# Layer 1's up products of the feed-forward: both parts of the state as one moving operand of 512 columns

## The chip, the cores and the metric

The kernel runs on one core of a Trainium2 chip. The metric is the device time of one execution in microseconds (us): the median of several runs. Three runs of the kernel before gave 1219.34, 1221.35 and 1221.39 us, median 1221.35.

## What is computed

Two layers of a block over 256 latent tokens (and, in layer 0 alone, 256 context tokens) of width 1024. Each layer mixes tokens in four branches and then applies a gated feed-forward, which is the part that the change touches:

```
def swiglu(h, w_up, w_down):
    a, u = jnp.split(h @ w_up, 2, axis=-1)
    return (jax.nn.silu(a) * u) @ w_down
```

with `w_up` of 1024 x 5632 and `w_down` of 2816 x 1024. Layer 1 is the last one: it has the 256 latent tokens only.

## The kernel before, in words

**Split numbers.** Products are taken in a reduced float format (fp32r), and accuracy is kept by splitting each operand x into a high part hi = x rounded to that format and a low part lo = x - hi. A product of w and h is then three products on TensorE into one PSUM bank: hi(w) hi(h), hi(w) lo(h), lo(w) hi(h) (`mm3`, lines 220 to 224). For a weight block the split is done on the chip: `_split` (line 97) issues a ScalarE copy for hi (line 102) and, through `flush` (line 108), a VectorE subtraction for lo (line 112).

**The up stage of layer 1** (`ffn`, line 1206, with T = 256 columns and NS = 1). The 5632 output channels are 44 blocks of 128: 22 gate blocks f (the half called a above) and 22 value blocks NF + f (the half called u). They are worked in pairs: gate block f, then value block NF + f. A block is 8 chunks k of 128 channels of the state; each chunk is one `mm3` with moving operands of 256 columns (`up_mm`, line 1222), so 24 products and 24 weight loads per block. The result lies in one of three PSUM banks that rotate (tag "b"). After a gate block `up_a` (line 1237) takes the sigmoid on ScalarE (line 1239) and multiplies on VectorE (line 1240); after a value block `up_u` (line 1243) multiplies on VectorE (sf, line 1246) and splits sf into shi on ScalarE (line 211) and slo on VectorE (line 212). The state of this stage is hm1: `new_h` (line 492) makes 8 tiles for its high parts and 8 for its low parts, 256 columns each, which `modulate` (line 472) fills. The first pair of blocks is worked chunk by chunk as the state comes (lines 1295 to 1302).

**The down stage** takes 22 blocks of 12 products of 512 columns each, on other PSUM banks, and reads shi and slo.

**Order.** Each engine works its instructions in the order in which the program issues them. The program is a list of steps; before each one the planner (`Weights.pump`, line 114) issues what is due of loads and splits, and then the step's own function runs:

```
            more = self.split_to(self.nth + ahead) or more
        assert all(b.raw is not None and (b.hi is not None or not b.split) for b in blocks)
```

```
    for n, st in enumerate(steps):
        weights.pump(n, st.blocks, st.ahead, st.lag)
        st.fn()
```

With `ahead` = 2, which all the steps of whole blocks have, the split of block n+2 (hi on ScalarE, lo on VectorE) is issued ahead of the products of block n and of what follows them. The split parts live in four ring buffers, the raw weights in four others, which SP's queue fills (line 94).

Of the kernel before, what the change touches and what calls it, by code (L numbers as in the profile page):

```python
# [8 lines left out]
F32 = mybir.dt.float32  # L9
F32R = mybir.dt.float32r  # L10
BF16 = mybir.dt.bfloat16
AF = mybir.ActivationFunctionType
ALU = mybir.AluOpType
# [4 lines left out]
P = 128  # L18
D = 1024
KC = D // P  # L20
# [6 lines left out]
NF = DFF // P  # L27
# [138 lines left out]
def kernel(ctx: ExitStack, tc: tile.TileContext, a: dict, out: bass.AP):  # L166
    ctx.enter_context(tc.manual_schedule())
    nc = tc.nc

    def pool(name, bufs=1, stack=ctx, **kw):  # L170
        return stack.enter_context(tc.tile_pool(name=name, bufs=bufs, reuse_waits="tile", **kw))
# [5 lines left out]
    hp = pool("hp")  # L177
# [5 lines left out]
    def bank(tag, name, shape=None, keep=False):  # L183

        i = banks[tag].pop(0)
        if not keep:
            banks[tag].append(i)
        t = psum.tile([P, 512], F32, tag=f"bank{i}", name=name)
        return t if shape is None else cut(t, shape)
# [4 lines left out]
    def cut(t, shape):  # L194
        n = 1
        for x in shape:
            n *= x
        t = t[:, :n]
        if len(shape) == 2:
            t = t.rearrange("p (a b) -> p a b", b=shape[1])  # L200
        if len(shape) == 3:
            t = t.rearrange("p (a b c) -> p a b c", b=shape[1], c=shape[2])
        return t
# [6 lines left out]
    def split(hi, lo, src):  # L210
        nc.scalar.activation(hi, src, AF.Copy)
        nc.vector.tensor_tensor(lo, src, hi.bitcast(F32), op=ALU.subtract)
# [7 lines left out]
    def mm3(ps, st, mv, first, last):  # L220

        nc.tensor.matmul(ps, lhsT=st[0], rhs=mv[0], start=first, stop=False)  # L222
        nc.tensor.matmul(ps, lhsT=st[0], rhs=mv[1], start=False, stop=False)  # L223
        nc.tensor.matmul(ps, lhsT=st[1], rhs=mv[0], start=False, stop=last)  # L224
# [265 lines left out]
            cut_lows()  # L490

    def new_h(T, name):
        return [
            [hp.tile([P, T], F32R, tag=f"h{x}{k}", name=f"{name}{x}{k}") for k in range(KC)]
            for x in ("hi", "lo")
        ]
# [709 lines left out]
    def ffn(l, h, hnext, before, chains):  # L1206
        T = 512 if l == 0 else 256
        NS = T // SEQ
        outer, early, late = ExitStack(), ExitStack(), ExitStack()
        P_ = {}  # L1210
# [9 lines left out]
        pps = {}  # L1220

        def up_mm(blk, b, cols, tag, ks=range(KC)):
            if b not in pps:
                pps[b] = bank(tag, f"up{l}{b}")[:, :T]
            for k in ks:
                sl = slice(k * P, (k + 1) * P)
                mm3(
                    pps[b][:, cols],
                    (blk.hi[:, sl], blk.lo[:, sl]),
                    (h[0][k][:, cols], h[1][k][:, cols]),  # L1230
                    k == 0,
                    k == KC - 1,
                )

        sgs = {}

        def up_a(f):
            sg = P_["t"].tile([P, T], F32, tag="sg", name="fsg")
            nc.scalar.activation(sg, pps[f], AF.Sigmoid)
            nc.vector.tensor_tensor(sg, sg, pps[f], op=ALU.mult)  # L1240
            sgs[f] = sg

        def up_u(f):
            sg, u = sgs.pop(f), pps[NF + f]
            sf = P_["t"].tile([P, SEQ], F32, tag="sf", name="sf")
            nc.vector.tensor_tensor(sf, sg[:, :SEQ], u[:, :SEQ], op=ALU.mult)
            if NS == 2:
                sc = P_["s"].tile([P, SEQ], F32, name=f"sc{f}")
                nc.vector.tensor_tensor(sc, sg[:, SEQ:], u[:, SEQ:], op=ALU.mult)
                sc_.append(sc)  # L1250
            hi = P_["s"].tile([P, SEQ], F32R, name=f"shi{f}")
            lo = P_["s"].tile([P, SEQ], F32R, name=f"slo{f}")
            split(hi, lo, sf)
            sh_.append(hi)
            sl_.append(lo)

        def up_block(b):
            return Block(a["w_up"][l, b], f"up{l}{b}")

        fs = list(range(NF))  # L1260
        if NS == 2:
# [3 lines left out]
            for n, (f, b, blk) in enumerate(first):  # L1265
                ks = range(KC) if n < 3 else range(KC // 2)
                steps.append(Step([blk], lambda blk=blk, b=b, ks=ks: up_mm(blk, b, lat, "a", ks), free=[]))
            _, b3, blk3 = first[3]
            do(at(turn, 0), lambda: up_mm(blk3, b3, lat, "a", range(KC // 2, KC)), before, begin)

            def up_end(f, b):
                (up_a if b == f else up_u)(f)

            def up_ctx(k0):
                for _, b, blk in first[:2]:
                    up_mm(blk, b, ctx_, None, (k0, k0 + 1))
# [13 lines left out]
        else:  # L1290
# [9 lines left out]
            steps[-1].ahead = 0  # L1300
            do(before, begin)
            steps.append(Step([], lambda: (up_a(0), up_u(0)), free=[blk for _, blk in first]))
            fs = fs[1:]
        for f in fs:
            for b in (f, NF + f):
                blk = up_block(b)

                def fn(f=f, b=b, blk=blk):
                    up_mm(blk, b, slice(0, T), "b")
                    (up_a if b == f else up_u)(f)  # L1310

                steps.append(Step([blk], fn))
# [58 lines left out]
    h = {}  # L1371

    def get_h(key, T):
        def fn():
            if key not in h:
                h[key] = new_h(T, f"h{key}")
            return h[key]

        return fn
# [190 lines left out]
    start = next(i for i, st in enumerate(mix0) if st.tick)  # L1570
    steps = mix0[:start] + weave(mix0[start:], cond_rows() + gate_steps_of(0, 0, 2) + mod_steps(0, 1, 2), 21, 46)

    class Later:
# [5 lines left out]
        def __getitem__(self, i):  # L1579
            return h[self.key][i]  # L1580

    ff0, end1 = ffn(0, Later("m0"), get_h("f0", 512), end0, ch0)
    both = gate_steps_of(0, 1, 2) + mod_steps(1, 0, 2)
    lat_only = mod_steps(1, 1, 1) + gate_steps_of(1, 0, 1) + gate_steps_of(1, 1, 1)
    steps += weave(ff0, cond_rows() + mixed(both, lat_only), 5, 60)
    mix1, end2, ch1 = mixer(1, Later("f0"), get_h("m1", 256))
    mix1.insert(0, Step([], end1, tick=False))
    steps += mix1
    ff1, end3 = ffn(1, Later("m1"), None, end2, ch1)
    steps += ff1  # L1590

# [104 lines left out]
```

## Time and profile before

| what | value |
|---|---|
| median of 3 runs | 1221.35 us |
| the profiled execution's own time | 1220.89 us |
| its span, first to last instruction | 1219.1 us |
| granted clock of TensorE, mean | 0.995 |
| TensorE busy | 98% of the span |
| VectorE busy | 783.1 us, 64% |
| ScalarE busy | 453.2 us, 37% |
| layer 1's up stage | about 1025 to 1152 us of the span |
| layer 1's down stage | about 1152 to 1212 us |

Times in rows are microseconds from the span's start. PE is TensorE (its products), PEld its weight loads, DVE VectorE, ACT ScalarE, SP the engine that issues transfers. "L112" is line 112 of the kernel; tiles go by the program's names, so `lo_up` is the low part of an up block and `fsg` the gate's result. Busy times of products overlap, because a product's row lasts from its first read to its modelled end: how fast TensorE goes is read from the steps between starts.

### The profile page before, as it was taken

The page shows a single profiled execution, that of the slowest core. Times are in us where ns is not written, and L with a number is a line of the kernel's source. Part 1 is how long each engine was busy: PE and PEld are TensorE (multiplying, and loading weights), DVE is VectorE, ACT ScalarE, POOL GpSimd, SP SyncE. Part 2 cuts the span into 40 slices and gives each one's busy share as a digit, 9 for nine tenths or more (in the row PEclk, how much of TensorE's full clock was granted, in tenths as well). Part 3 has the DMA queues.
Part 4 walks back from the last instruction along what each step waited for, and adds up shares of the span by engine and source line. Part 5 has one row for each costly group of instructions (what it writes and reads, how often), then busy time and mean ns, then how long its engine had stood idle before and what let it go on. Part 6 is the DMA issues. An engine that isn't in the chain of part 4 may idle for free.

```text
span 1219.1 us, 17611 instructions
## 1 busy us (share of the span) xinstructions
PE 1189.1 (98%) x6960; PEld 1028.8 (84%) x6960; DVE 783.1 (64%) x1275; ACT 453.2 (37%) x715; POOL 41.7 (3%) x39
## 2 busy tenths in 40 slices
PE   7999999999999989999999999989989999999997
PEld 5987778888888878888888888889879998999986
DVE  5464745586875656775777673576666666666644
ACT  4332323323222643222322222564334445444442
POOL 1500000000000100000000000000000000000000
PEclk9999999999999999999999999999999999999999
DMA  8642325457565225666666773334455663665662
GB/s 290 233 131 70 112 87 190 150 180 172 183 194 161 67 104 170 210 204 169 233 204 215 245 234 97 130 111 160 125 155 163 199 233 112 191 183 181 201 214 86
DMA packets 66435, 205.67 MB, mean 169 GB/s; under 512 B 14640, under 2 KB 18480, under 8 KB 66352
## 3 DMA queue, kind: packets, MB, share of 16 engines
q1 hardware_dynamic: 65776, 204.39, 53.6%
q8 instruction: 55, 0.90, 0.3%
q14 instruction: 28, 0.23, 0.1%
q10 hardware_dynamic: 576, 0.16, 0.1%
HBM read 203.41 MB, written 1.11 MB: 168 GB/s over the span
## 4 chain that ended last, share of the span: by engine, by line
PE 87%; DVE 5%; ACT 4%; DMA 2%; issue 2%; POOL 1%; SPq 0%; DVEq 0%; POOLq 0%; ACTq 0%
PE up L223 10%; PE up L224 10%; PE up L222 10%; PE gate L222 7%; PE gate L224 7%; PE gate L223 7%; PE dn L224 4%; PE dn L223 4%; PE dn L222 4%; PE pb L224 2%; PE pb L223 2%; PE pb L222 2%; PE wo L224 1%; ACT junk L443 1%; PE wo L223 1%
## 5 line engine op out<-in xcount | busy, mean ns | idle before, releaser
L338 DVE SCALAR_TENSOR_TENSOR mjunk<-raw_mod,crow 128x1024 bf16<-128x1024 f32 x128 | 156.4, 1222 | 8.8 <-DMA raw_mod<-in_w_modt 6.8
L223 PE MATMUL up<-hm0lo,hi_up 128*128 128x512 f32 (+1 forms) x384 | 143.5, 374 | 2.8 <-DVE hm0lo L470 2.8
L224 PE MATMUL up<-hm0hi,lo_up 128*128 128x512 f32 (+1 forms) x384 | 143.2, 373 | 2.5 <-DVE lo_up L112 2.5
L222 PE MATMUL up<-hm0hi,hi_up 128*128 128x512 f32 (+1 forms) x384 | 143.5, 374 | 0.0
L112 DVE TENSOR_TENSOR lo_up<-raw_up,hi_up 128x1024 fp32r<-128x1024 f32 x88 | 107.6, 1223 | 36.6 <-ACT hi_up L102 36.5
L112 DVE TENSOR_TENSOR lo_gt<-raw_gt,hi_gt 128x1280 fp32r<-128x1280 f32 x64 | 95.3, 1489 | 31.4 <-ACT hi_gt L102 31.4
L222 PE MATMUL gate<-h0hi,hi_gt 128*128 128x512 f32 x256 | 100.6, 393 | 0.0
L222 PE MATMUL up<-hm1hi,hi_up 128*128 128x256 f32 x352 | 99.8, 284 | 0.0
L223 PE MATMUL up<-hm1lo,hi_up 128*128 128x256 f32 x352 | 99.7, 283 | 0.1
L223 PE MATMUL gate<-h0lo,hi_gt 128*128 128x512 f32 x256 | 99.6, 389 | 0.0
L224 PE MATMUL gate<-h0hi,lo_gt 128*128 128x512 f32 x256 | 99.6, 389 | 0.0
L224 PE MATMUL up<-hm1hi,lo_up 128*128 128x256 f32 x352 | 99.6, 283 | 0.0
L102 ACT ACTIVATE hi_up<-raw_up 128x1024 fp32r<-128x1024 f32 x88 | 92.2, 1049 | 9.5 <-DMA raw_up<-in_w_up 8.9
L102 ACT ACTIVATE hi_gt<-raw_gt 128x1280 fp32r<-128x1280 f32 x64 | 81.0, 1265 | 21.1 <-DMA raw_gt<-in_w_gate 21.0
L112 DVE TENSOR_TENSOR lo_dn<-raw_dn,hi_dn 128x1024 fp32r<-128x1024 f32 x44 | 53.6, 1224 | 54.1 <-ACT hi_dn L102 54.1
L223 PEld LDWEIGHTS up<-hm0lo,hi_up 128*128 128x128 f32 x384 | 72.8, 190 | 16.0 <-DVE hm0lo L470 3.7
L224 PEld LDWEIGHTS up<-hm0hi,lo_up 128*128 128x128 f32 x384 | 72.9, 190 | 15.3 <-DVE lo_up L112 2.7
L1065 ACT ACTIVATE sg<-gate 128x512 f32<-128x512 f32 (+1 forms) x64 | 31.3, 488 | 143.6 <-PE gate L224 143.5
L222 PEld LDWEIGHTS up<-hm0hi,hi_up 128*128 128x128 f32 x384 | 72.9, 190 | 12.5
L102 ACT ACTIVATE hi_dn<-raw_dn 128x1024 fp32r<-128x1024 f32 x44 | 46.4, 1058 | 91.8 <-PE dn L224 68.3
L222 PE MATMUL gate<-hf0hi,hi_gt 128*128 128x256 f32 x256 | 73.5, 287 | 0.0
L223 PE MATMUL gate<-hf0lo,hi_gt 128*128 128x256 f32 x256 | 72.4, 283 | 0.0
(342 smaller groups left out, 2718.3 us busy)
## 6 DMA issues: line engine op xcount, KB each, us to landing
raw_up<-in_w_up SPq DMA_DIRECT2D x88, 512.0 KB, 3.9
raw_gt<-in_w_gate SPq DMA_DIRECT2D x64, 640.0 KB, 3.9
raw_mod<-in_w_modt SPq DMA_DIRECT2D x80, 512.0 KB, 4.1
raw_dn<-in_w_down SPq DMA_DIRECT2D x44, 512.0 KB, 4.3
raw_in<-in_w_in SPq DMA_DIRECT2D x28, 512.0 KB, 3.7
raw_wo<-in_w_o SPq DMA_DIRECT2D x16, 512.0 KB, 4.1
raw_mod<-in_w_mod SPq DMA_DIRECT2D x12, 512.0 KB, 5.2
grow<-gscr SPq DMA_DIRECT2D x6, 512.0 KB, 7.2
```

What stands on the lines that cost most here:

```text
L102: self.nc.scalar.activation(b.hi, b.raw, AF.Copy)
L112: self.nc.vector.tensor_tensor(b.lo, b.raw, b.hi.bitcast(F32), op=ALU.subtract)
L222: nc.tensor.matmul(ps, lhsT=st[0], rhs=mv[0], start=first, stop=False)
L223: nc.tensor.matmul(ps, lhsT=st[0], rhs=mv[1], start=False, stop=False)
L224: nc.tensor.matmul(ps, lhsT=st[1], rhs=mv[0], start=False, stop=last)
L338: nc.vector.scalar_tensor_tensor(junk, b.raw, 1.0, crow[s], op0=ALU.mult, op1=ALU.mult, accum_out=out()[:, s, i : i + 1])
L443: nc.scalar.activation(junk, src, AF.Square, scale=1.0 / 32.0, accum_out=acc)
L1065: nc.scalar.activation(sg, ps, AF.Sigmoid)
```

## The change

In layer 1 alone, the high and the low part of each state chunk become the two halves of one tile of 512 columns (`new_h`). A chunk is then two products: hi(w) with all 512 columns into a whole PSUM bank, and lo(w) with the 256 columns of the high part into the bank's first half; in the last chunk in the other order. The bank's second half thus holds hi(w) lo(h) by itself, and `up_sum` adds the halves: a ScalarE copy of the second half into SBUF and a VectorE addition of the first. The sigmoid and both multiplications then read the sum in SBUF instead of PSUM. Layer 0 keeps its products.

```diff
     def new_h(T, name):
+        if name == "hm1":
+
+            hl = [hp.tile([P, 2 * T], F32R, tag=f"hhi{k}", name=f"{name}{k}") for k in range(KC)]
+            return [[x[:, :T] for x in hl], [x[:, T:] for x in hl], hl]
         return [
...
         def up_mm(blk, b, cols, tag, ks=range(KC)):
             if b not in pps:
-                pps[b] = bank(tag, f"up{l}{b}")[:, :T]
+                pps[b] = bank(tag, f"up{l}{b}")
             for k in ks:
                 sl = slice(k * P, (k + 1) * P)
+                if NS == 1:
+                    run = [(pps[b], blk.hi, h[2][k]), (pps[b][:, :T], blk.lo, h[0][k])]
+                    for n, (ps, w, x) in enumerate(run[::-1] if k == KC - 1 else run):
+                        nc.tensor.matmul(ps, lhsT=w[:, sl], rhs=x, start=k == 0 and n == 0, stop=k == KC - 1 and n == 1)
+                    continue
                 mm3(
...
+        def up_sum(b):
+
+            if NS == 2:
+                return pps[b]
+            x = P_["t"].tile([P, T], F32, tag="us", name="fus")
+            nc.scalar.activation(x, pps[b][:, T:], AF.Copy)
+            nc.vector.tensor_tensor(x, x, pps[b][:, :T], op=ALU.add)
+            return x
+
         def up_a(f):
+            x = up_sum(f)
             sg = P_["t"].tile([P, T], F32, tag="sg", name="fsg")
-            nc.scalar.activation(sg, pps[f], AF.Sigmoid)
-            nc.vector.tensor_tensor(sg, sg, pps[f], op=ALU.mult)
+            nc.scalar.activation(sg, x, AF.Sigmoid)
+            nc.vector.tensor_tensor(sg, sg, x, op=ALU.mult)
             sgs[f] = sg
 
         def up_u(f):
-            sg, u = sgs.pop(f), pps[NF + f]
+            sg, u = sgs.pop(f), up_sum(NF + f)
```

## Rows read from the trace of the kernel before

**Rows 1.** The page: span, and each engine's busy us (share) and instructions.

```profile
span 1219.1 us, 17611 instructions
...
PE 1189.1 (98%) x6960; PEld 1028.8 (84%) x6960; DVE 783.1 (64%) x1275; ACT 453.2 (37%) x715; POOL 41.7 (3%) x39
```

**Rows 2.** Windows, up stage: us, busy PE, PEld, DVE, ACT, POOL, clock, DMA share, GB/s.

```profile
1031.10:1152.40 121.30, 121.30 (x1013) 121.30 (x1012) 79.14 (x107) 56.92 (x85) 0.00 (x0) 1.00 0.62 186
```

**Rows 3.** Timeline of PE in layer 0's up stage: start, duration, line, operation.

```profile
559.76 0.39 PE L222 MATMUL up<-hm0hi,hi_up 128*128 128x512 f32 x1
...
569.96 0.39 PE L222 MATMUL up<-hm0hi,hi_up 128*128 128x512 f32 x1
```

**Rows 4.** Timeline of PE where 512 columns are followed by 256.

```profile
416.35 0.39 PE L224 MATMUL wo<-hi_wo,ml 128*128 128x512 f32 x1
416.58 0.28 PE L222 MATMUL up<-hm0hi,hi_up 128*128 128x256 f32 x1
416.70 0.28 PE L223 MATMUL up<-hm0lo,hi_up 128*128 128x256 f32 x1
```

**Rows 5.** Groups by line, 880 us to the end: count, busy us, mean ns, idle before.

```profile
L223 PEld LDWEIGHTS up<-hm1lo,hi_up 128*128 128x128 f32 x352 | 67.6, 192 | 0.3 <-DVE hm1lo L470 0.3
```

**Rows 6.** Timeline of DVE, one pair of blocks; brackets hold idle time and its releaser.

```profile
1034.17 1.23 DVE L112 TENSOR_TENSOR lo_up<-raw_up,hi_up 128x1024 fp32r<-128x1024 f32 x1 [0.53 <-ACT hi_up L102]
1035.31 0.42 DVE L1240 TENSOR_TENSOR fsg<-fsg,up 128x256 f32<-128x256 f32 x1
1035.91 1.23 DVE L112 TENSOR_TENSOR lo_up<-raw_up,hi_up 128x1024 fp32r<-128x1024 f32 x1 [0.19 <-ACT hi_up L102]
1037.43 0.42 DVE L1246 TENSOR_TENSOR sf<-fsg,up 128x256 f32<-128x256 f32 x1 [0.29 <-PE up L224]
1038.34 0.43 DVE L212 TENSOR_TENSOR slo<-sf,shi 128x256 fp32r<-128x256 f32 x1 [0.48 <-ACT shi L211]
1039.29 1.23 DVE L112 TENSOR_TENSOR lo_up<-raw_up,hi_up 128x1024 fp32r<-128x1024 f32 x1 [0.52 <-ACT hi_up L102]
```

**Rows 7.** Timeline of ACT over the same pair.

```profile
1034.55 0.38 ACT L1239 ACTIVATE fsg<-up 128x256 f32<-128x256 f32 x1 [0.41 <-PE up L224]
1034.83 1.05 ACT L102 ACTIVATE hi_up<-raw_up 128x1024 fp32r<-128x1024 f32 x1
1037.89 0.42 ACT L211 ACTIVATE shi<-sf 128x256 fp32r<-128x256 f32 x1 [2.00 <-DVE sf L1246]
1038.21 1.04 ACT L102 ACTIVATE hi_up<-raw_up 128x1024 fp32r<-128x1024 f32 x1
```

**Rows 8.** Timeline of DVE in layer 1's mixer, an operation that reads the last one's result.

```profile
945.55 0.41 DVE L1074 TENSOR_TENSOR sg<-sg,pb 128x256 f32<-128x256 f32 x1
946.00 0.43 DVE L1075 TENSOR_TENSOR mg<-mg,sg 128x256 f32<-128x256 f32 x1
```

**Rows 9.** Timelines of PE and DVE at the start of layer 1's up stage.

```profile
1025.31 0.38 PE L223 MATMUL up<-hm1lo,hi_up 128*128 128x256 f32 x1
...
1031.80 0.41 DVE L1240 TENSOR_TENSOR fsg<-fsg,up 128x256 f32<-128x256 f32 x1
1032.32 0.42 DVE L1246 TENSOR_TENSOR sf<-fsg,up 128x256 f32<-128x256 f32 x1
```

**Rows 10.** Timelines at the start of the down stage: DVE's lo, PE in block three.

```profile
1154.49 3.50 DVE L112 TENSOR_TENSOR lo_dn<-raw_dn,hi_dn 128x1024 fp32r<-128x1024 f32 x3 [0.53 <-ACT hi_dn L102]
...
1158.12 0.39 PE L223 MATMUL dn<-lo_dn,shi 128*128 128x512 f32 x1
```

**Rows 11.** DMA issues, 1030 to 1150 us: count, KB each, median us to landing.

```profile
raw_up<-in_w_up SPq DMA_DIRECT2D x38, 512.0 KB, 3.7
```

**Rows 12.** Windows as in rows 2, and PE's timeline in a stretch at half clock.

```profile
816.34 0.41 PE L223 MATMUL bg<-hf0lo,hi_in 128*128 128x256 f32 x1
...
818.47 0.41 PE L224 MATMUL bg<-hf0hi,lo_in 128*128 128x256 f32 x1
...
890.00:900.00 10.00, 8.66 (x70) 7.64 (x70) 6.40 (x13) 6.72 (x13) 0.00 (x0) 1.00 0.50 115
```

## The prediction

> **What bounds the kernel now.** I read the page first, then the stretch of layer 1's feed-forward cut out by time, then the timelines of the three engines that work in it. The page says that TensorE is busy for 98% of the span [rows 1]. In the stretch from 1031.1 to 1152.4 us, where 42 of the 44 up blocks of layer 1 are multiplied, it is busy all the time at the full granted clock (1.00, so 2.4 GHz), while VectorE has 79.1 us of work and ScalarE 56.9 us [rows 2]. So this stage is bound by TensorE today, and one is tempted to ask only what the change does to TensorE. The busy shares hide what matters here: VectorE and ScalarE work in the order of the program and hand work to each other, so that their chain can be much longer than either one's busy time.
>
> **TensorE's part of the change.** Today a chunk k of a block takes three products of 256 columns; after it, one of 512 and one of 256. The number of columns is the same (768). 1013 products of 256 columns fill 121.3 us [rows 2], 0.120 us each; 256 columns at 2.4 GHz are 0.1067 us, so 0.013 us of each is a fixed part. Products of 512 columns follow each other at (569.96 - 559.76)/45 = 0.2267 us (46 records, the two shown are the first and the last) [rows 3], which is 0.2133 + 0.013: the fixed part is per product, not per column. Where 512 columns are followed by 256 the steps are 0.23 and 0.12 us [rows 4], so mixing costs nothing that the row shows. A chunk goes from 3 x 0.120 = 0.360 to 0.2267 + 0.120 = 0.347 us, a block of eight from 2.88 to 2.77 us, and the 352 chunks [rows 5] save 352 x 0.0133 = **4.7 us of TensorE**. The bounds: nothing (a 512-column product at twice 0.120), and 352 x 0.120 = 42 us if a product's whole step went away, which the 0.2267 us of rows 3 exclude.
>
> 352 weight loads go too. Each row of one lasts 192 ns [rows 5], but it lies beside a product: with steps of 0.120 us there is no room for it outside. So I price a removed load at nothing beyond the 0.013 us above. The Trainium skill ("TensorE: Matmul & The Clock Gate", part 3, on what overlaps) says that a weight load overlaps products in flight only where it goes to another row group, which these full-size loads don't; with its price for a load, 128 columns at 1.2 GHz or 107 ns, TensorE would save 38 us by estimate. The steps of 0.120 us for products whose columns alone take 0.107 speak against it.
>
> **What is added on the other two engines.** Per block: a ScalarE copy of 128x256 from PSUM, and a VectorE addition of 128x256 with one operand in PSUM. The nearest rows are sf, a VectorE operation with the same kinds of operands (0.42 us) [rows 6], the sigmoid, which reads the same shape from PSUM (0.38), and the shi copy (0.42) [rows 7]. In busy time VectorE goes from 79.1/42 = 1.88 to 2.30 us a block, still under TensorE's 2.77. By busy time the addition would be hidden. It is not, because of where it stands in the queues.
>
> **The order in the queues.** At step n the planner first issues the split of block n+2 (hi on ScalarE, lo on VectorE, at once), then the products of block n, then what follows block n. The rows show it: lo, mult, lo, sf, slo, lo on VectorE [rows 6], and sigmoid, hi, shi, hi on ScalarE [rows 7]. Today the sigmoid waits for TensorE alone, so for a gate block ("a") the next hi doesn't depend on VectorE. For a value block ("u") it does: sf, shi, hi, lo. After the change it does **for every block**: the addition of block n stands on VectorE behind lo of block n+2; the sigmoid (a) or sf and shi (u) need its result; hi of block n+3 stands on ScalarE behind them; lo of n+3 needs that hi. The loop closes: lo(n+2), add(n), sigmoid or shi(n), hi(n+3), lo(n+3). The copy is outside of the loop, since ScalarE does it while lo runs.
>
> Its length, start to start:
> - lo to the next VectorE operation that waits for nothing: 1034.17 to 1035.31, 1.14 us [rows 6].
> - A VectorE result to a ScalarE start: sf 1037.43 to shi 1037.89, 0.46 us [rows 6, 7], taken for add to sigmoid too.
> - add to sf, both on VectorE, the second reading the first's result: 945.55 to 946.00, 0.45 us [rows 8]; the other end is 1031.80 to 1032.32, 0.52 us [rows 9].
> - sigmoid to hi 0.28 us, shi to hi 0.32 [rows 7]. The sigmoid will read SBUF as shi does, so 0.32 for both.
> - hi to lo: 1034.83 to 1035.91 and 1038.21 to 1039.29, 1.08 us [rows 6, 7].
>
> While the addition waits for lo, everything of its block stands behind it on VectorE, the next lo too, and TensorE waits for that one. A gate block: 1.14 + 0.46 + 0.32 + 1.08 = 3.00 us. A value block: 1.14 + 0.45 + 0.46 + 0.32 + 1.08 = 3.45 us. **A pair: 6.45 us**, against 5.54 us that TensorE needs for it after the change and 5.76 today. The same sum for today is 1.14 + 0.46 + 0.32 + 1.08 = 3.0 for the value block, and for the gate block 1.14 + 0.42, so 4.6 us a pair: hidden under 5.76. For the ends of the pair I take 6.30 (the sigmoid to hi at 0.28, and each hand-over a little shorter) and 6.65 (0.52 instead of 0.45, and as much more at two other hand-overs).
>
> **The sum.** The multiplication behind blocks 0 and 1 starts at 1031.80 [rows 9]; the first addition will start in its place (VectorE is busy with lo until then). Then sigmoid 1032.26, mult 1032.7, the second addition 1033.1, sf 1033.5, shi 1034.0, hi 1034.3, lo of block 4 at 1035.4, done at 1036.6. TensorE, done with blocks 0 and 1 at about 1031.1 (the start of the stretch [rows 2]), needs it two blocks later, at 1031.1 + 5.54 = 1036.6; from block 6 on it waits for the loop. Lo runs two blocks ahead, so the loop covers 21 pairs until lo of the third down block: 1035.4 + 21 x 6.45 = 1170.9, done 1.23 later, at 1172.1 us. Today the product that needs it (the second of that block) starts at 1158.12, long after its lo, which starts at 1154.49 [rows 10]. So the down products, and all behind them, start 14.0 us later. From there on VectorE has only one lo per 12 x 0.2267 = 2.72 us, and catches up. The profiled execution took 1220.9 us, 0.5 below the median of the three runs; 1220.9 + 14.0 = **1234.9, forecast 1235 us**. With 6.30 and 6.65 a pair the delay is 10.8 and 18.2 us: 1231.7 to 1239.1.
>
> The other edits. The state's parts in one tile: the very first product now waits for the low part, where only the second did, at 1025.31 [rows 9]; the wider product then ends where the second one does today, so nothing, and if that cover is gone at most that product's 0.38 us. A PSUM bank is free after the addition instead of after the product with it, and three banks rotate; TensorE waits for lo anyway, so nothing, and at most one VectorE operation, 0.42 us, per block once lo came early. Weight loads from memory land in 3.7 us for a block [rows 11] and there are four buffers for a block each 3.2 us: nothing, and SP's queue keeps its order.
>
> **The rivals.**
> 1. *The loop doesn't close, and TensorE stays the bound: faster.* It needs a pair under 5.54 us, that is additions that run ahead of lo on VectorE, or 0.9 us less in the hand-overs. For it: busy time alone (2.30 us a block) leaves room. Against it: the order in rows 6, where nothing overtakes a waiting lo. Time: 1220.9 - 4.7 = 1216 us. Chance 0.08. In 0.01 of these the loads removed are worth their whole row, 352 x 0.192 = 68 us [rows 5], which the steps of 0.120 speak against: 1153 us. The Trainium skill's rule above would put this case at 1183 us.
> 2. *The loop closes at TensorE's pace,* about 5.6 to 5.9 us a pair, because hand-overs are shorter or the fixed part of a product isn't saved: from -3 to +2 us, about 1221. Chance 0.04.
> 3. *TensorE's clock falls as well.* It will wait some 0.45 us in each 3.2. At 1.2 GHz a 256-column product takes (818.47 - 816.34)/10 = 0.213 us [rows 12], a block 8 x (0.427 + 0.213) = 5.1 us instead of 2.77, more than the loop. Were half of 40 blocks so, 20 x (5.1 - 3.2) = 38 us more: 1273 us; one block in eight, 10 us more, 1245. Against it: between 890 and 900 us TensorE was busy for 8.66 of 10 us, and the granted clock stayed at 1.00 [rows 12]. Chance 0.08, mostly at its lower end.
> 4. The forecast: 0.80.
>
> **Numbers.** 0.2% is 2.4 us, about what a measurement of this kernel can tell from no change. Faster 0.09 (rival 1 and a bit of 2), same 0.03 (the rest of 2), slower 0.88 (forecast and 3). The range takes the loop from just under 6.2 to 6.8 a pair, and leaves out rivals 1, 2 and the upper part of 3: 1228 to 1243 us.
>
> **What the next profile would show.** Right: TensorE's products of the up stage at steps of 0.227 and 0.12, but with a wait before nearly every block, put down to lo_up; VectorE idle before lo (for hi) and ScalarE idle before the sigmoid (for the addition); lo_up at alternating steps of 3.0 and 3.45 us; the stage some 14 us longer and the down stage as long as before. Wrong: no waits of TensorE for lo_up (rival 1), or a granted clock under 1 between 1040 and 1165 us (rival 3). A longer or shorter pair with the same waits would mean that a hand-over was mispriced.

## The result and the profile after

The changed kernel takes 1234.07 us, the median of four runs (1233.47 to 1234.67); the kernel before has a median of 1220.34 us over its four runs. The ratio is 1.0113, with a 95% interval of 1.01 to 1.0125: 13.7 us slower. The forecast was 1235.

The page of the changed kernel, its span and the busy line, as in [rows 1]:

```profile
span 1232.7 us, 16951 instructions
...
PE 1195.5 (97%) x6607; PEld 1007.4 (82%) x6608; DVE 797.8 (65%) x1319; ACT 465.4 (38%) x759; POOL 41.6 (3%) x39
```

The span has grown by 13.6 us, as the time has. VectorE and ScalarE have 14.7 and 12.2 us more of work spread over a stage of some 140 us, and neither is near full. The answer is not in this line. Who waited for whom between 1040 and 1165 us (total us, times, longest us):

```profile
...
ACT fsg L1258 <- DVE fus L1252: 25.8, 19, 1.4
PEld up L1234 <- DVE lo_up L112: 22.2, 38, 0.8
DVE lo_up L112 <- ACT hi_up L102: 20.0, 38, 0.5
DVE slo L212 <- ACT shi L211: 9.7, 20, 0.5
...
PE up L1234 <- DVE lo_up L112: 7.0, 18, 0.4
```

Two of these are new. The sigmoid (fsg) waits for VectorE's sum (fus), where it used to wait for TensorE. And TensorE waits for lo_up before 38 blocks, most plainly at its weight load. Now VectorE's timeline over one pair of blocks, to be laid beside [rows 6]:

```profile
1041.40 1.23 DVE L112 TENSOR_TENSOR lo_up<-raw_up,hi_up 128x1024 fp32r<-128x1024 f32 x1 [0.53 <-ACT hi_up L102]
1042.55 0.41 DVE L1252 TENSOR_TENSOR fus<-fus,up 128x256 f32<-128x256 f32 x1
1043.45 0.42 DVE L1259 TENSOR_TENSOR fsg<-fsg,fus 128x256 f32<-128x256 f32 x1 [0.48 <-ACT fsg L1258]
1044.40 1.23 DVE L112 TENSOR_TENSOR lo_up<-raw_up,hi_up 128x1024 fp32r<-128x1024 f32 x1 [0.53 <-ACT hi_up L102]
1045.54 0.41 DVE L1252 TENSOR_TENSOR fus<-fus,up 128x256 f32<-128x256 f32 x1
1045.99 0.42 DVE L1265 TENSOR_TENSOR sf<-fsg,fus 128x256 f32<-128x256 f32 x1
1046.90 0.42 DVE L212 TENSOR_TENSOR slo<-sf,shi 128x256 fp32r<-128x256 f32 x1 [0.48 <-ACT shi L211]
1047.85 1.23 DVE L112 TENSOR_TENSOR lo_up<-raw_up,hi_up 128x1024 fp32r<-128x1024 f32 x1 [0.53 <-ACT hi_up L102]
```

and ScalarE's over the same pair, as in [rows 7]:

```profile
1043.00 0.42 ACT L1258 ACTIVATE fsg<-fus 128x256 f32<-128x256 f32 x1 [1.36 <-DVE fus L1252]
1043.32 1.04 ACT L102 ACTIVATE hi_up<-raw_up 128x1024 fp32r<-128x1024 f32 x1
1044.27 0.36 ACT L1251 ACTIVATE fus<-up 128x256 f32<-128x256 f32 x1
1046.45 0.42 ACT L211 ACTIVATE shi<-sf 128x256 fp32r<-128x256 f32 x1 [1.81 <-DVE sf L1265]
1046.77 1.05 ACT L102 ACTIVATE hi_up<-raw_up 128x1024 fp32r<-128x1024 f32 x1
```

Follow one turn: lo 1041.40, sum 1042.55, sigmoid 1043.00, hi 1043.32, lo 1044.40. Every start lies within 0.1 us of the end of the one before it, on the other engine or on the same, and TensorE is in none of them. The copy out of PSUM (1044.27) starts as soon as hi is through, some 1.3 us ahead of the sum that reads it. A gate block's turn is 3.00 us, a value block's (1044.40 to 1047.85) 3.45.

The stage as a whole, and the clock in it (windows, columns as in [rows 2]):

```profile
1031.10:1164.00 132.90, 125.91 (x672) 99.45 (x671) 90.31 (x147) 67.73 (x125) 0.00 (x0) 1.00 0.54 165
```

TensorE idles for 7.0 us of it by its busy share. The busy share understates the wait, since a product's row reaches past the step to the next one; what was lost is in the steps. The granted clock stayed at full level in it (1.00). The loop's first and last turn, and the product that needs the last one, as in [rows 10]:

```profile
1034.97 1.23 DVE L112 TENSOR_TENSOR lo_up<-raw_up,hi_up 128x1024 fp32r<-128x1024 f32 x1 [0.52 <-ACT hi_up L102]
...
1170.28 4.63 DVE L112 TENSOR_TENSOR lo_dn<-raw_dn,hi_dn 128x1024 fp32r<-128x1024 f32 x4 [0.52 <-ACT hi_dn L102]
...
1171.56 0.50 PE L223 MATMUL dn<-lo_dn,shi 128*128 128x512 f32 x1 [0.39 <-DVE lo_dn L112]
```

From lo of the fifth block to lo of the third down block are 21 pairs: (1170.28 - 1034.97)/21 = 6.44 us a pair. The second product of the third down block starts at 1171.56 instead of 1158.12 [rows 10], 13.4 us later. The last down product starts at 1225.63 instead of 1212.07 us, 13.6 later: behind that point only 0.1 us more is lost.

### The profile page after: what moved, and what is told of

Its sections match the earlier page's. It is cut to its first block, busy times and chain, and to the rows that moved or that the text cites. A ratio compares the mean times of both kernels' runs of the same rounds, so it can differ in the third digit from the quotient of the medians.

```text
span 1232.7 us, 16951 instructions
## 1 busy us (share of the span) xinstructions
PE 1195.5 (97%) x6607; PEld 1007.4 (82%) x6608; DVE 797.8 (65%) x1319; ACT 465.4 (38%) x759; POOL 41.6 (3%) x39
## 4 chain that ended last, share of the span: by engine, by line
PE 76%; DVE 11%; ACT 8%; issue 2%; DMA 2%; POOL 1%; SPq 0%; DVEq 0%; POOLq 0%; ACTq 0%
PE gate L222 7%; PE gate L223 7%; PE gate L224 7%; PE up L223 6%; PE up L224 6%; PE up L222 6%; DVE lo_up L112 4%; PE dn L224 4%; PE dn L223 4%; PE dn L222 4%; ACT hi_up L102 3%; PE pb L222 2%; PE pb L223 2%; PE pb L224 2%; PE wo L224 1%
## 5 line engine op out<-in xcount | busy, mean ns | idle before, releaser
L1234 PE MATMUL up<-hm,hi_up 128*128 128x512 f32 x352 | 123.1, 398 | 0.0
L1234 PE MATMUL up<-hm,lo_up 128*128 128x256 f32 x352 | 95.8, 293 | 7.0 <-DVE lo_up L112 7.0
L1234 PEld LDWEIGHTS up<-hm,lo_up 128*128 128x128 f32 x352 | 66.9, 190 | 24.3 <-DVE lo_up L112 22.2
```

The lines of the kernel that those rows point to most:

```text
L1234: nc.tensor.matmul(ps, lhsT=w[:, sl], rhs=x, start=k == 0 and n == 0, stop=k == KC - 1 and n == 1)
```

## The experiments

The theory is the closed loop of the forecast: lo(n+2), sum(n), sigmoid or shi(n), hi(n+3), lo(n+3). Its rivals in the runs were that the added work slows the stage by its amount, wherever it stands (rival A), and that the wide products are slower beside the other engines' work (rival B).

**1. The order alone.** The same instructions; only the split of block n+3 (hi and lo) is issued ahead of ScalarE's next operation on block n instead of behind it: between the sum and the sigmoid for a gate block, between sf and shi for a value block.

```diff
         def up_a(f, between=lambda: None):
             x = up_sum(f)
+            between()
             sg = P_["t"].tile([P, T], F32, tag="sg", name="fsg")
...
             nc.vector.tensor_tensor(sf, sg[:, :SEQ], u[:, :SEQ], op=ALU.mult)
+            between()
...
                     up_mm(blk, b, slice(0, T), "b")
-                    (up_a if b == f else up_u)(f)
+                    early = (lambda: weights.split_to(blk.nth + 3)) if NS == 1 else (lambda: None)
+                    (up_a if b == f else up_u)(f, early)
```

> The same instructions as the changed kernel; only the split of block n+3 (hi and lo) is issued between the sum of block n and the sigmoid or shi that read it. Theory (closed loop lo, add, sigmoid or shi, hi, lo): hi no longer stands behind the sigmoid or shi, and lo no longer behind a wait for them, so VectorE and ScalarE run freely, TensorE is the bound again at 2.77 us a block, and the time is 4.7 us under the kernel before, about 1215.6 us. Rival A (the added work itself, its busy time and its reads of PSUM, slows the stage wherever it stands): stays at about 1234. Rival B (the wider products are themselves slower beside the other engines' work): stays well above 1220.

Measured: 1217.58 us beside 1220.63 of the kernel before, ratio 0.9972 (0.9963 to 0.9981). A second time, on another chip: 1217.55 beside 1220.73, ratio 0.9973 (0.9963 to 0.9982).

> The reordered kernel once more, unchanged, beside the grouped one on the same chip: 1217.6 us as before, to read the difference of the two within one job.

VectorE's timeline in the reordered kernel, a pair of blocks:

```profile
1044.84 1.22 DVE L112 TENSOR_TENSOR lo_up<-raw_up,hi_up 128x1024 fp32r<-128x1024 f32 x1 [0.52 <-ACT hi_up L102]
1045.98 0.42 DVE L1260 TENSOR_TENSOR fsg<-fsg,fus 128x256 f32<-128x256 f32 x1
1046.65 0.42 DVE L1252 TENSOR_TENSOR fus<-fus,up 128x256 f32<-128x256 f32 x1 [0.25 <-ACT fus L1251]
1047.10 0.42 DVE L1266 TENSOR_TENSOR sf<-fsg,fus 128x256 f32<-128x256 f32 x1
1047.60 1.23 DVE L112 TENSOR_TENSOR lo_up<-raw_up,hi_up 128x1024 fp32r<-128x1024 f32 x1
1048.74 0.42 DVE L212 TENSOR_TENSOR slo<-sf,shi 128x256 fp32r<-128x256 f32 x1
```

and ScalarE's copies behind two value blocks:

```profile
1046.23 0.38 ACT L1251 ACTIVATE fus<-up 128x256 f32<-128x256 f32 x1 [1.12 <-PE up L1234]
...
1051.87 0.38 ACT L1251 ACTIVATE fus<-up 128x256 f32<-128x256 f32 x1 [1.12 <-PE up L1234]
```

The multiplication and slo now stand right behind lo and wait for nothing. VectorE still waits 0.52 us for hi behind a gate block's sum, but that hi no longer waits for VectorE: it follows the copy, and the copy waits for TensorE. TensorE has no wait for lo_up left between 1020 and 1170 us. So nothing but the place of each block's hi and lo in their two queues turned 13.7 us of loss into 3 us of gain. The added work itself, all of it still there, is hidden: rival A falls. The gain is short of the 4.7 us expected: a pair takes 1051.87 - 1046.23 = 5.64 us, not 5.54.

**2. The wide products alone**, without the sum:

```diff
         def up_sum(b):
             if NS == 2:
                 return pps[b]
+            return pps[b][:, :T]
```

> TensorE's half of the change alone: the products of 512 and 256 columns as in the changed kernel, but the second half of the bank is never read, the sigmoid and the multiplications read the first half as before (hi(w) lo(h) is left out of the sum). Theory: no loop, and the fixed 0.013 us of 352 products is saved: 4.7 us under the kernel before, about 1215.6 us. Rival A (added work): the same, since the work is gone. Rival B (the wider products are slower): no gain or a loss, 1220 or more.

Measured: 1218.18 us, ratio 0.9981 (0.9972 to 0.999). TensorE is the bound, and its pace is read over four blocks, from one block's end to that of the fourth after it:

```profile
1090.08 0.40 PE L1234 MATMUL up<-hm,lo_up 128*128 128x256 f32 x2
...
1101.36 0.40 PE L1234 MATMUL up<-hm,lo_up 128*128 128x256 f32 x2
```

(1101.36 - 1090.08)/4 = 2.82 us a block, 0.3525 a chunk. The products do win against 2.88, but 44 x 0.06 = 2.6 us and not 4.7. So this term of the forecast was mis-sized; the loop kept it off the path there.

**3. The sum alone**, with the products of before: the copy takes the block's result, and the maximum of copy and result is that result.

```diff
+        def up_sum(b):
+
+            if NS == 2:
+                return pps[b]
+            x = P_["t"].tile([P, T], F32, tag="us", name="fus")
+            nc.scalar.activation(x, pps[b], AF.Copy)
+            nc.vector.tensor_tensor(x, x, pps[b], op=ALU.max)
+            return x
```

> The other half alone: the kernel before with its three products of 256 columns, plus a ScalarE copy of the block's result and a VectorE operation on the copy and the result (maximum of the two, which is the result), in the place where the changed kernel has copy and addition. Theory: the same loop of 6.45 us a pair, above TensorE's 5.76 us, so the same time as the changed kernel, 1233 to 1235 us. Rival B (wider products): as the kernel before, 1220 us. With waits of TensorE for lo_up of about 0.35 us a block instead of 0.45.

Measured: 1234.19 us, ratio 1.011 (1.0093 to 1.0127): the time of the changed kernel, without its products. Two lo of VectorE, one pair apart:

```profile
1100.02 1.23 DVE L112 TENSOR_TENSOR lo_up<-raw_up,hi_up 128x1024 fp32r<-128x1024 f32 x1 [0.52 <-ACT hi_up L102]
...
1106.46 1.23 DVE L112 TENSOR_TENSOR lo_up<-raw_up,hi_up 128x1024 fp32r<-128x1024 f32 x1 [0.53 <-ACT hi_up L102]
```

6.44 us again. The whole loss comes with the detour through copy and sum, and 0.06 us a block more on TensorE (2.88 instead of 2.82) doesn't show in the time. Rival B falls.

**4 and 5. The sum behind half of the blocks.** The two kernels add the same number of instructions. By the theory the sum lengthens a value block's part of the loop by 0.45 us (3.00 to 3.45), but a gate block's by 1.44 (1.56 to 3.00), because it makes the sigmoid wait for VectorE.

```diff
             if NS == 2:
                 return pps[b]
+            if b < NF:
+                return pps[b][:, :T]
```

(run 4, value blocks alone; run 5, gate blocks alone, has `b >= NF`)

> The changed kernel with copy and addition behind value blocks alone; behind gate blocks the sigmoid and the multiplication read the bank's first half (hi(w) lo(h) is left out of the gate). Theory (closed loop): the gate block's sigmoid needs nothing from VectorE again, its part of the loop falls from 3.00 to 1.56 us, a pair takes 5.0 us, under TensorE's 5.64 (two blocks of 2.82, the step measured where TensorE is the bound), so the time is that of the wide products without a sum, 1218 us. Rival A (the added work slows the stage by its amount): half of the work, half of the loss, 1226 to 1227.

> The changed kernel with copy and addition behind gate blocks alone; behind value blocks the multiplication reads the bank's first half (hi(w) lo(h) is left out of the value half). As many added instructions as in the run with value blocks alone. Theory: gate block 3.00 us as in the changed kernel, value block 1.14 + 0.46 + 0.32 + 1.08 = 3.00 us as before the change, a pair 6.0 us against TensorE's 5.64: lo of the third down block is done at about 1162 us where TensorE wants it at 1158, some 4 us more than the kernel before, 1224 to 1225 us. Rival A (amount of work): the same time as with value blocks alone, 1226 to 1227.

Measured: behind value blocks 1217.88 us, ratio 0.9983 (0.9972 to 0.9995); behind gate blocks 1224.43 us, ratio 1.0035 (1.0018 to 1.0052), 4.5 us more than the kernel before. VectorE with the sum behind value blocks, two sums one pair apart:

```profile
1100.10 0.42 DVE L1254 TENSOR_TENSOR fus<-fus,up 128x256 f32<-128x256 f32 x1 [0.64 <-ACT fus L1253]
...
1105.74 0.42 DVE L1254 TENSOR_TENSOR fus<-fus,up 128x256 f32<-128x256 f32 x1 [0.64 <-ACT fus L1253]
```

5.64 us, TensorE's pace, with 0.64 us of slack ahead of the sum. With the sum behind gate blocks, three lo in a row:

```profile
1100.42 1.22 DVE L112 TENSOR_TENSOR lo_up<-raw_up,hi_up 128x1024 fp32r<-128x1024 f32 x1 [0.53 <-ACT hi_up L102]
...
1103.41 1.22 DVE L112 TENSOR_TENSOR lo_up<-raw_up,hi_up 128x1024 fp32r<-128x1024 f32 x1 [0.52 <-ACT hi_up L102]
...
1106.40 1.23 DVE L112 TENSOR_TENSOR lo_up<-raw_up,hi_up 128x1024 fp32r<-128x1024 f32 x1 [0.53 <-ACT hi_up L102]
```

2.99 us each, 5.98 a pair, as worked out. Equal work, 6.6 us apart: what counts is where the sum stands.

**6 and 7. One more operation, inside the loop and beside it.** One VectorE addition per block whose result nobody reads, ahead of the sum (run 6, the edit shown), or the same line behind the gate's multiplication and behind slo (run 7).

```diff
             nc.scalar.activation(x, pps[b][:, T:], AF.Copy)
+            nc.vector.tensor_tensor(P_["t"].tile([P, T], F32, tag="jk", name="jk"), h[0][0].bitcast(F32), h[0][1].bitcast(F32), op=ALU.add)
             nc.vector.tensor_tensor(x, x, pps[b][:, :T], op=ALU.add)
```

> The changed kernel with one more VectorE addition of 128x256 per block, on two chunks of the state in SBUF, its result unread, issued just ahead of the sum's addition, that is inside the loop. Theory: each block's turn of the loop grows by the 0.33 us at which such operations follow each other, a pair by 0.67 us, 21 pairs by 14 us: 1248 us. Rival A (amount of work): 44 more operations cost the same here as behind the chain.

> The changed kernel with the same extra VectorE addition per block, issued behind the gate's multiplication and behind slo, that is into the 0.5 us in which VectorE waits for the next hi. Theory: it fits into that wait, lo starts when it did, and the time stays that of the changed kernel, 1234 us within 1. Rival A (amount of work): as much more as with the operation ahead of the addition.

Measured: inside 1248.52 us, ratio 1.0242 (1.0226 to 1.0258); beside 1233.99 us, ratio 1.0118 (1.0101 to 1.0135). VectorE in run 6:

```profile
1102.76 1.23 DVE L112 TENSOR_TENSOR lo_up<-raw_up,hi_up 128x1024 fp32r<-128x1024 f32 x1 [0.52 <-ACT hi_up L102]
1103.90 0.42 DVE L1252 TENSOR_TENSOR jk<-hm,hm 128x256 f32<-128x256 f32 x1
1104.24 0.41 DVE L1253 TENSOR_TENSOR fus<-fus,up 128x256 f32<-128x256 f32 x1
...
1109.86 1.22 DVE L112 TENSOR_TENSOR lo_up<-raw_up,hi_up 128x1024 fp32r<-128x1024 f32 x1 [0.53 <-ACT hi_up L102]
```

and in run 7:

```profile
1102.22 0.42 DVE L1259 TENSOR_TENSOR fsg<-fsg,fus 128x256 f32<-128x256 f32 x1 [0.48 <-ACT fsg L1258]
1102.56 0.42 DVE L1262 TENSOR_TENSOR jk<-hm,hm 128x256 f32<-128x256 f32 x1
1103.17 1.22 DVE L112 TENSOR_TENSOR lo_up<-raw_up,hi_up 128x1024 fp32r<-128x1024 f32 x1 [0.19 <-ACT hi_up L102]
```

In run 6 the operation costs its step, 1104.24 - 1103.90 = 0.34 us a block, and a pair takes 7.10 us: 14.5 us more than the changed kernel. In run 7 it eats 0.34 of the 0.53 us for which VectorE waits, and lo starts 0.95 us behind the multiplication, as it did in the changed kernel (1043.45 to 1044.40). 44 operations of 0.42 us cost 14 us or nothing.

**8. Where the products' missing 2 us are.** The reordered kernel with each block's wide products first, its narrow ones behind them.

```diff
+            if NS == 1:
+                for k in ks:
+                    nc.tensor.matmul(pps[b], lhsT=blk.hi[:, k * P : (k + 1) * P], rhs=h[2][k], start=k == 0, stop=False)
+                for k in ks:
+                    ps = pps[b][:, :T]
+                    nc.tensor.matmul(ps, lhsT=blk.lo[:, k * P : (k + 1) * P], rhs=h[0][k], start=False, stop=k == KC - 1)
+                return
```

> The reordered kernel (split of block n+3 between the sum and what reads it) with the products of a block grouped by width: its eight of 512 columns first, then its eight of 256. It asks where the wide products' missing gain is: a chunk took 0.3525 us where TensorE was the bound, not 0.347. Theory C (changing width in every chunk costs it): in groups the steps are 0.2267 and 0.120 again, a block takes 2.77 us, 44 blocks save 44 x 0.05 = 2.2 us: 1215.4 us. Theory D (a wide product costs 0.233 us in this stage whatever stands beside it): no change, 1217.6 us.

Measured: 1217.68 us, ratio 0.9971 (0.9961 to 0.9981), beside 1217.55 of run 1 on the same chip: no difference that these times can tell. TensorE's timeline, from one block to the next and to the 16th after the first:

```profile
1091.04 2.00 PE L1231 MATMUL up<-hm,hi_up 128*128 128x512 f32 x8
1092.88 1.11 PE L1234 MATMUL up<-hm,lo_up 128*128 128x256 f32 x8
1093.84 2.00 PE L1231 MATMUL up<-hm,hi_up 128*128 128x512 f32 x8
...
1135.74 2.00 PE L1231 MATMUL up<-hm,hi_up 128*128 128x512 f32 x8
```

A block takes (1135.74 - 1091.04)/16 = 2.794 us: eight wide steps of (1092.88 - 1091.04)/8 = 0.230 and eight narrow ones of 0.12. Against 2.82 the grouping gives back 0.026 us a block, 1.1 us over the stage, which is too little to see in the times. So the change of width in every chunk accounts for about half of the 0.05 us a block that were missing, and theory C for no more than that. Theory D doesn't fit either, since a wide step in a group is 0.230 and not 0.233 us, and it names no cause.

## Why the prediction was right

- **The closed loop** was the forecast's main claim, and runs 1 to 7 show it from both sides: it opens by order alone, it comes with the sum alone, it scales with what stands in it (7.10, 6.44, 5.98 us a pair, or TensorE's 5.64 where the loop is shorter), and it doesn't notice what stands beside it.
- **The pair** was put at 6.45 us and measures 6.44. All of its terms were rows of the kernel before: lo to the next operation 1.15 (1.14 forecast), sum to sigmoid 0.45 (0.46), sum to sf 0.45 (0.45), sigmoid to hi 0.32 (0.32), hi to lo 1.08 (1.08). Of the two choices that were open, 0.32 against 0.28 had a reason (the sigmoid reads SBUF as shi does); 0.45 against 0.52 had none and fell right by luck, worth 0.07 x 21 = 1.5 us.
- **Where the loop starts and ends**: lo of block 4 was put at 1035.4 and came at 1034.97. 0.38 of these 0.43 us were there at the first sum already (1031.42 instead of 1031.80); the traces of runs 3, 6 and 7 put that sum at 1032.07, 1031.58 and 1031.88, so this is scatter between executions. The last lo that counts was to be done at 1172.1, and the product behind it started at 1171.56. The delay was put at 14.0 us and is 13.4 at that product, 13.7 in the times. An agreement within 0.3 us is closer than the forecast's own 10.8 to 18.2 us promised, and in part luck.
- **TensorE's part**: 4.7 us of saving were forecast; runs 2, 4, 1 and 8 show 2 to 3, and the steps 2.6. The sentence that failed is that mixing costs nothing that the row shows [rows 4]: rows of two decimals don't show 0.006 us, and there was one row. With the loop in charge it changed nothing, but rival 1 would have been at 1218 us and not 1216.
- **Rival 1** is what the reordered kernel does: the loop doesn't close, and the change is a gain. The condition that the forecast named for it, additions ahead of lo or 0.9 us less in the hand-overs, was too narrow: in run 1 the sum still stands behind an lo and sum to sf takes 0.45 us as before (1046.65 to 1047.10), but hi no longer stands behind the sum's readers. **Rival 2** didn't come: the pair took 6.44 us, not 5.6 to 5.9. **Rival 3**: the clock stayed at full level from 1031 us to the end of the stage although TensorE waited before nearly every block. Ahead of that the granted clock was 0.50 (the 1.2 GHz level) from 1024 to 1026 us, in the first pair of blocks, where the profiled execution of the kernel before had 1.00. This isn't the loss: run 7's trace has 1.00 there, and its time is the changed kernel's.
- **The weight loads** were priced at nothing of their own, and run 2 agrees: with a weight load less per chunk TensorE saved 2.6 us by its steps. By the Trainium skill's rule on what overlaps ("TensorE: Matmul & The Clock Gate", part 3) it would have been 38 us by estimate; run 2 doesn't bear that out.
- The other edits cost nothing that the trace shows: no wait for a PSUM bank or for a load from memory stands among the waits between 1040 and 1165 us.

## What to carry to other kernels

An operation's busy time says what it costs only if its engine is the bound; where two engines hand work to each other in program order, add up the starts around the loop, and compare that sum with the pace of the engine that you believe is the bound. Before adding a step that makes one queue wait for the other, issue the independent long work (here the next split) ahead of the instruction that waits, not behind it. The same two sums per pair cost 13.7 us against the kernel before with the split behind their readers (the changed kernel), and nothing beside run 2 with the split ahead of them (run 1).

## What the runs showed of the hardware that was not expected

A wide product took 0.2267 us in layer 0 [rows 3], but 0.23 or more among narrow ones. The longer step is there in the kernel before as well, at the start of the down stage, right behind the narrow products of the up stage:

```profile
1152.43 0.40 PE L222 MATMUL dn<-hi_dn,shi 128*128 128x512 f32 x1
...
1153.82 0.39 PE L222 MATMUL dn<-hi_dn,shi 128*128 128x512 f32 x1
...
1160.84 0.39 PE L223 MATMUL dn<-lo_dn,shi 128*128 128x512 f32 x1
```

The first six steps are (1153.82 - 1152.43)/6 = 0.232 us, the next 31 are (1160.84 - 1153.82)/31 = 0.2265. But narrow neighbours are not needed for it. In the changed kernel's second down block it comes back 4.5 us behind the last narrow product, right behind a product that had waited for lo_dn:

```profile
1168.45 0.40 PE L224 MATMUL dn<-hi_dn,slo 128*128 128x512 f32 x1
...
1170.77 0.39 PE L222 MATMUL dn<-hi_dn,shi 128*128 128x512 f32 x1
```

These are ten steps of wide products alone, (1170.77 - 1168.45)/10 = 0.232 us each. In the up stage of the changed kernel, where TensorE pauses before each block, chunks took 0.348 us within a block, nearer to the 0.347 forecast than the 0.3525 of the kernels in which it never pauses:

```profile
1101.24 0.39 PE L1234 MATMUL up<-hm,hi_up 128*128 128x512 f32 x1
...
1102.63 0.39 PE L1234 MATMUL up<-hm,hi_up 128*128 128x512 f32 x1
```

(four chunks, 1.39 us). So a pause goes with shorter steps in one place and with longer ones in the other, and neither the neighbours nor the pause by itself sorts these rows. No run tried more, and the cause stays open.
